# Down projections as Strassen block products in a two-block network

## The chip, the cores and the metric

The kernel runs on one core of one Trainium2 chip. The metric is the time of one execution on the device in microseconds (us). TensorE (PE in the rows; PEld is its weight load) multiplies matrices, VectorE (DVE), ScalarE (ACT) and GpSimd (POOL) work element by element, and SyncE (SP) issues the transfers. All weights come from device memory once per use; SBUF holds the operands and PSUM the sums of the matmuls.

## The reference

Two transformer blocks run one behind the other over 528 tokens (16 learned ones and 512 of the input) of width 1024. The first has two layers of mixed attention and a gated feed-forward net, the second one layer of sparse attention and a gated feed-forward net. The change concerns only the last product of each of the three feed-forward nets, the down projection from 2816 to 1024:

```python
def conv_ffn(x, w_up, conv_w, conv_b, w_down):
    h = x @ w_up
    ...
    u, g = jnp.split(hc, 2, axis=-1)
    return (jax.nn.silu(g) * u) @ w_down
...
h = h + conv_ffn(rms_norm(h, ffn_norm[i]), w_up[i], conv_w[i], conv_b[i], w_down[i])
...
h = h + (jax.nn.silu(f @ w_gate[i]) * (f @ w_up[i])) @ w_down[i]
```

Everything is float32.

## The kernel before

**Layout.** Features lie on the 128 partitions and tokens along the free axis. The residual h is eight tiles of 128 x 528; a feed-forward net has 22 tiles of 128 hidden features. Every operand of a matmul is split into a rounded part (hi) and a remainder (lo), and a product is three passes: hi by hi, hi by lo, lo by hi.

**Jobs.** The work on TensorE is a list of jobs. A job makes one block of 128 output features: `steps` (L304) runs over its K row blocks of the weights, and for each issues the three passes (L322) over the tokens. In layer 0 the tokens are two halves of 264 (`FULL`), each a matmul of its own with its own weight load; where the first 16 tokens are not needed, one matmul has all 512 (`SEQT`). The sum stands in one of two PSUM buffers `mm` and the job's `evac` takes it out. `load` (L247) brings weights for two jobs (a chunk `raw`, up to 1024 rows by 256 columns, 1 MB) into one of two buffers. `split` (L258) makes hi on ACT (L273) and lo on DVE (L274) from it; `run` (L337) calls it two jobs ahead of the job that needs it, and weights have three buffers each.

**The feed-forward nets.** The 22 hidden tiles are taken in thirds (`THIRDS`, L34: 8, 7 and 7 tiles). The order of jobs is: up projections of the first third and four jobs of the second, down projection of the first third, the rest of the second and four jobs of the last, down projection of the second third, the rest, down projection of the last third. A down projection of one third is a down phase here: eight jobs with K = 7 or 8, one per tile of h, each added to h by one DVE operation (L1035 in the layers, L1452 in block 2). After the last phase of a layer each tile of h is also scaled into the next stage's operands (L182, L193) and its squares are added up on POOL (L204). An up job ends with an evacuation with the norm's factor (L378), in the layers a convolution (L992 on ACT, L994 and L995 on DVE), the gate (L1006, L1008) and hi and lo of the product (L1010, L179); in block 2 with a gate on ACT (L1420) and POOL (L1421). In block 2 the last third is done twice, over 256 tokens each (the last stage: 16 jobs, L1470 takes out the sums, L1480 adds squares on POOL), so that one half's output work runs beside the other's matmuls.

**What sets the order.** The Python code is in program order, evacuations have a high priority, and a scheduler fixes each engine's queue when the program is built. Each engine then runs its queue strictly in order and waits at its head. The profile names tiles by their base: raw, wh, wl (weights), g (any 128 x 528 tile), mm (PSUM).

## Time and profile before

| what | value |
|---|---|
| median of 3 runs | 2361.13 us (2360.93 to 2361.45) |
| profiled execution | 2361.31 us |
| its span, first to last instruction | 2359.5 us |
| PE busy | 2318.5 us (98%) |
| VectorE busy | 1378.4 us (58%) |
| ScalarE busy | 952.2 us (40%) |
| GpSimd busy | 248.3 us (11%) |
| mean granted TensorE clock | 0.992 of full speed |
| read from device memory | 192.26 MB |

Busy times are sums over the span. Matmuls overlap in the pipeline, so PE counts as busy through most of the span, and the distance between starts is what one costs. The groups of instructions name the line, the tiles, the shapes and the number, the busy time, the mean duration of one, and the idle time of the engine ahead of them with what ended it. The table of stretches has one line for each stretch of the span: its length, the busy time and the number of instructions of PE, PEld, DVE, ACT and POOL in this order, the granted clock, the share of the transfer engines and their rate; its last line is the sum over the stretches asked for.

### The profile page before, as it was taken

What the parts mean: (1) busy time and instruction counts of PE and PEld (TensorE: products, weight loads), DVE (VectorE), ACT (ScalarE), POOL (GpSimd) and SP (SyncE); (2) the same over time, 40 slices, a digit from 0 to 9 for tenths busy, and PEclk for the clock granted to TensorE, in tenths of its full rate; (3) what the DMA queues carried; (4) which work ended last, traced back from release to release, by engine and by line L of the source; (5) the groups of instructions that cost most, each with busy time, mean ns of one, the idle gap of its engine ahead of it and who ended that gap; (6) DMA issues with size and microseconds to landing.
All of it is one profiled execution on the core that took longest, in us unless ns stands there. A gap on an engine that the chain in (4) does not pass through costs nothing.

```text
span 2359.5 us, 37628 instructions
## 1 busy us (share of the span) xinstructions
PE 2318.5 (98%) x15703; PEld 2133.4 (90%) x15703; DVE 1378.4 (58%) x2480; ACT 952.2 (40%) x1641; POOL 248.3 (11%) x261
## 2 busy tenths in 40 slices
PE   7999999999999999999999999999999999999998
PEld 6999999999998998999998889988999888888888
DVE  6667556465556677466464666797454454333335
ACT  6555434233346655343242544322233533222225
POOL 3111210000021112200000121100000002101012
PEclk9999999999999999999999999999999999999999
DMA  4211122222231211222223222222212222232323
GB/s 115 73 55 55 55 90 90 90 90 89 96 87 54 55 55 54 90 90 90 90 84 105 85 76 88 90 90 90 89 55 72 72 90 90 92 105 89 98 85 130
DMA packets 217072, 196.77 MB, mean 83 GB/s; under 512 B 8987, under 2 KB 214791, under 8 KB 216903
## 3 DMA queue, kind: packets, MB, share of 16 engines
q1 hardware_dynamic: 216903, 194.37, 25.9%
q8 instruction: 124, 2.03, 0.3%
q14 instruction: 45, 0.37, 0.1%
HBM read 192.26 MB, written 2.10 MB: 82 GB/s over the span
## 4 chain that ended last, share of the span: by engine, by line
PE 66%; ACT 1%; DVE 1%; issue 1%; POOL 0%; DMA 0%; POOLq 0%; ACTq 0%; SPq 0%
PE mm L322 59%; PE valuesT L1158 1%; PE scoresS L1141 1%; PE foxV L620 1%; PE attend_pT L480 1%; PE foxT L600 0%; ACT wh L273 0%; PE foxS L510 0%; POOL g L204 0%; PE spreadS L223 0%; PE foxS L511 0%; PE idx L510 0%; DMA raw<-in_w_down_dram 0%; PE to_tokensT L463 0%; PE idx L511 0%
## 5 line engine op out<-in xcount | busy, mean ns | idle before, releaser
L322 PE MATMUL mm<-g,wh 128*128 128x264 f32 (+3 forms) x9168 | 1883.0, 316 | 13.8 <-DVE g L378 11.7
L322 PEld LDWEIGHTS mm<-g,wh 128*128 128x128 f32 x9168 | 1393.3, 190 | 113.8 <-issue 12.8
L322 PE MATMUL mm<-g,wl 128*128 128x264 f32 (+3 forms) x4552 | 1161.0, 313 | 0.0
L322 PEld LDWEIGHTS mm<-g,wl 128*128 128x128 f32 x4552 | 752.2, 189 | 50.4
L273 ACT ACTIVATE wh<-raw 128x1024 fp32r<-128x1024 f32 (+1 forms) x369 | 384.9, 1043 | 947.9 <-PE mm L322 808.8
L274 DVE TENSOR_TENSOR wl<-raw,wh 128x1024 fp32r<-128x1024 f32 (+1 forms) x369 | 445.1, 1206 | 66.0 <-ACT wh L273 55.8
L378 DVE TENSOR_TENSOR g<-mm,g 128x528 f32<-128x528 f32 (+2 forms) x228 | 158.5, 696 | 318.7 <-PE mm L322 315.4
L204 POOL TENSOR_TENSOR g<-g,g 128x528 f32<-128x528 f32 (+3 forms) x49 | 71.4, 1469 | 914.9 <-ACT g L203 568.0
L179 DVE TENSOR_TENSOR g<-g,g 128x512 fp32r<-128x512 f32 (+3 forms) x131 | 92.1, 703 | 38.2 <-ACT g L1010 29.0
L1035 DVE TENSOR_TENSOR g<-mm,g 128x528 f32<-128x528 f32 (+1 forms) x48 | 33.6, 700 | 119.3 <-PE mm L322 119.3
L992 ACT ACTIVATE g<-g,cv 128x528 f32<-128x528 f32 (+1 forms) x88 | 72.1, 819 | 17.8 <-DVE g L378 17.7
L1421 POOL TENSOR_TENSOR g<-g,g 128x512 f32<-128x512 f32 x22 | 38.9, 1766 | 283.9 <-ACT g L1420 283.9
L995 DVE SCALAR_TENSOR_TENSOR g<-g,cv,g 128x526 f32<-128x526 f32 (+1 forms) x88 | 66.9, 760 | 3.1
L994 DVE SCALAR_TENSOR_TENSOR g<-g,cv,g 128x527 f32<-128x527 f32 (+1 forms) x88 | 66.3, 754 | 1.8 <-ACT g L992 1.8
L179 DVE TENSOR_TENSOR g<-foxT,g 128x128 fp32r<-128x128 f32 (+1 forms) x160 | 50.5, 340 | 20.3 <-ACT g L605 18.0
L1006 ACT ACTIVATE g<-g 128x528 f32<-128x528 f32 (+1 forms) x44 | 28.1, 639 | 84.0 <-DVE g L995 84.0
L1008 DVE TENSOR_TENSOR g<-g,g 128x528 f32<-128x528 f32 (+1 forms) x44 | 30.8, 701 | 32.4 <-ACT g L1006 32.4
L575 ACT ACTIVATE g<-g,sm 128x144 f32<-128x144 f32 (+2 forms) x80 | 43.1, 538 | 16.0 <-DVE sm L571 15.3
L187 POOL TENSOR_TENSOR sm<-sm,mhalf 128x10 f32<-128x10 f32 (+3 forms) x29 | 37.2, 1290 | 115.2 <-DVE sm L186 114.9
L605 ACT ACTIVATE g<-foxT 128x256 fp32r<-128x256 f32 (+1 forms) x96 | 33.1, 345 | 27.6 <-PE foxT L600 22.5
L1010 ACT ACTIVATE g<-g 128x528 fp32r<-128x528 f32 (+1 forms) x44 | 28.1, 638 | 33.1 <-DVE g L1008 33.1
L1452 DVE TENSOR_TENSOR g<-mm,g 128x512 f32<-128x512 f32 x16 | 11.1, 692 | 49.9 <-PE mm L322 49.9
(282 smaller groups left out, 1706.8 us busy)
## 6 DMA issues: line engine op xcount, KB each, us to landing
raw<-in_w_up_dram SPq DMA_DIRECT2D x50, 1024.0 KB
raw<-in_w_in_dram SPq DMA_DIRECT2D x44, 1024.0 KB
raw<-in_w_down_dram SPq DMA_DIRECT2D x28, 896.0 KB
raw<-in_w_in_dram SPq DMA_DIRECT2D x28, 512.0 KB
raw<-in_w_out_dram SPq DMA_DIRECT2D x12, 1024.0 KB
raw<-in_w_down_dram SPq DMA_DIRECT2D x12, 1024.0 KB
raw<-in_w_gate_dram SPq DMA_DIRECT2D x10, 1024.0 KB
raw<-in_w_up_dram SPq DMA_DIRECT2D x10, 512.0 KB
```

What stands on the lines that cost most here:

```text
L179: (eng or self.nc.vector).tensor_tensor(out, x, hi.bitcast(F32), op=ALU.subtract)
L187: self.nc.gpsimd.tensor_tensor(out, v[:rows, :n], self.mhalf[:rows, :n], op=ALU.pow)
L204: nc.gpsimd.tensor_tensor(acc[:, t0:t1], tmp[:, t0:t1], acc[:, t0:t1], op=ALU.add)
L273: keep(nc.scalar.activation(hi[:, :K], src, AF.Copy))
L274: keep(nc.vector.tensor_tensor(lo[:, :K], src, hi[:, :K].bitcast(F32), op=ALU.subtract))
L322: nc.tensor.matmul(ps[:, b, :n], lhsT=w[:, k, :], rhs=x[:, t:t + n], start=(ki == 0 and pi == 0), stop=(ki == len(order) - 1 and pi == len ...
L378: self.nc.vector.tensor_tensor(self.v(out, toks), self.psv(ps, toks), self.v(rs, toks), op=ALU.mult)
L575: nc.scalar.activation(P[:qs, :N], P[:qs, :N], AF.Exp, scale=-1.0, bias=m, accum_out=col)
L992: nc.scalar.activation(A[:, lo:], U[:, lo:], AF.Identity, bias=self.vec("cb", 44 * i + t), scale=cw(2))
L994: nc.vector.scalar_tensor_tensor(A[:, s1:], U[:, s1 - 1:L - 1], cw(1), A[:, s1:], op0=ALU.mult, op1=ALU.add)
L995: nc.vector.scalar_tensor_tensor(A[:, s0:], U[:, s0 - 2:L - 2], cw(0), A[:, s0:], op0=ALU.mult, op1=ALU.add)
L1421: nc.gpsimd.tensor_tensor(z[:, META:], z[:, META:], self.rs[:, META:], op=ALU.mult)
```

## The change

The down projections of all phases but block 2's last stage are done on pairs of output blocks. For two column blocks (128 features each), a pair of row blocks and the two token halves A and B, the 2 x 2 block product takes seven block products in place of eight. Line numbers of this section are those of the changed kernel.

- `THIRDS` is now 8, 8 and 6 tiles, so that row blocks pair up. Block 2's last stage keeps the plain form, with 6 row blocks.
- Weights: `split_product` makes the sums of weight blocks once per chunk: s1 on DVE (L279), s3 in place in `raw` and s2 and s4 on POOL (L280 to L282), then for each of the products 1, 6, 5, 7, 4, 2, 3 hi on ACT (L287) and lo on DVE (L288), each of n x 128 columns with n = 4 (or 3 in the third of 6).
- Hidden tiles: `seven` (L291) makes four differences of each tile pair (L296 to L299; on POOL, for the very last pair on DVE) and splits b11, t1 to t4, b21 and b22 (L301 to L308; the lo parts are L183).
- Products: `pair_steps` (L313) issues 3 n matmuls per product over one token half (L332), into PSUM tiles mmS (products 1, 6 and 4) and mm (5 with 7, 2 with 3). Sums of products are added to the two tiles h1 and h2 of the residual by ACT (L344), DVE with a PSUM input (L347, L349, L354, L357, L360) and POOL (L345, L350, L351).
- `run` (L448) cuts products ahead as long as six weight buffers hold them, and loads up to two chunks ahead. A job of the other kind takes two of the six buffers.
- Unchanged operations stand at other lines: L179, L182, L204, L274, L378, L994, L995 and L1008 of before are L183, L186, L208, L378, L516, L1132, L1133 and L1146 now.

```diff
-THIRDS = [list(range(0, 8)), list(range(8, 15)), list(range(15, 22))]
+THIRDS = [list(range(0, 8)), list(range(8, 16)), list(range(16, 22))]
+WTILES = 6
+
+PRODS = {1: ("a11", "b11"), 6: ("s2", "t2"), 5: ("s1", "t1"), 7: ("s3", "t3"), 4: ("a22", "t4"),
+         2: ("a12", "b21"), 3: ("s4", "b22")}
...
+    def split_product(self, jb, q):
...
+            nc.vector.tensor_tensor(s1, a21, a22, op=ALU.add)
+            nc.gpsimd.tensor_tensor(a21, a21, a11, op=ALU.add)
+            nc.gpsimd.tensor_tensor(s2, a21, a22, op=ALU.add)
+            nc.gpsimd.tensor_tensor(s4, s2, a12, op=ALU.add)
+            jb["left"] = dict(a11=a11, a12=a12, a22=a22, s1=s1, s2=s2, s3=a21, s4=s4)
+        src = jb["left"][PRODS[q][0]]
...
+        nc.scalar.activation(hi, src, AF.Copy)
+        nc.vector.tensor_tensor(lo, src, hi.bitcast(F32), op=ALU.subtract)
...
+    def seven(self, f1, f2, t0, n, eng):
...
+        eng.tensor_tensor(t12[:, :n], f1[:, B], f1[:, A], op=ALU.subtract)
+        eng.tensor_tensor(t12[:, n:2 * n], f2[:, B], t12[:, :n], op=ALU.subtract)
+        eng.tensor_tensor(t34[:, n:2 * n], f2[:, A], t12[:, n:2 * n], op=ALU.subtract)
+        eng.tensor_tensor(t34[:, :n], f1[:, B], f2[:, B], op=ALU.subtract)
...
+    def pair_steps(self, jb, prods):
...
+        for k in range(len(rhs)):
+            for q in prods:
+                hi, lo = jb["w"][q]
+                xh, xl = rhs[k][PRODS[q][1]]
+                for pi, (w, x) in enumerate(((hi, xh), (hi, xl), (lo, xh))):
+                    nc.tensor.matmul(z[q], lhsT=w[:, k, :], rhs=x, start=k == 0 and pi == 0,
+                                     stop=k == len(rhs) - 1 and pi == 2)
...
+                if q == 1:
+                    z["u"], z["v"] = self.G(), self.G()
+                    nc.scalar.activation(z["u"][:, :n], z[1], AF.Copy)
+                    nc.gpsimd.tensor_tensor(h1[:, A], h1[:, A], z["u"][:, :n], op=ALU.add)
+                elif q == 6:
+                    nc.vector.tensor_tensor(z["v"][:, :n], z[6], z["u"][:, :n], op=ALU.subtract)
+                elif q == 5:
+                    nc.vector.tensor_tensor(z["v"][:, n:2 * n], z[5], z["v"][:, :n], op=ALU.add)
+                    nc.gpsimd.tensor_tensor(h2[:, t0:t0 + 2 * n], h2[:, t0:t0 + 2 * n], z["v"][:, :2 * n], op=ALU.add)
+                    nc.gpsimd.tensor_tensor(h1[:, B], h1[:, B], z["v"][:, n:2 * n], op=ALU.subtract)
+                elif q == 7:
+                    hv = h2[:, t0:t0 + 2 * n].rearrange("p (a b) -> p a b", a=2)
+                    nc.vector.tensor_tensor(hv, z[7].unsqueeze(1).to_broadcast([128, 2, n]), hv, op=ALU.add)
...
+    def units(self, jb):
+
+        if not jb.get("pair"):
+            return [(jb, None, 1 if jb.get("packed") else 2)]
+        groups = [[1, 6, 5, 7], [2], [3], [4]] if jb.get("first") else [[q] for q in PRODS]
+        return [(jb, g, len(g)) for g in groups]
```

**DVE's queue in a full down phase.** The queue of VectorE in the first down phase of layer 0, before: one evacuation (L1035) and one split (L274) per job.

```order
L1035 TENSOR_TENSOR g29_216<-mm948_5436,g29_216 128x528
L274 TENSOR_TENSOR wl950_5487<-raw938_5320,wh949_5486 128x1024
L1035 TENSOR_TENSOR g36_234<-mm951_5490,g36_234 128x528
L274 TENSOR_TENSOR wl954_5543<-raw945_5430,wh953_5542 128x1024
L1035 TENSOR_TENSOR g42_254<-mm955_5546,g42_254 128x528
```

The same phase of the changed kernel, between two L347 (of the third and the fourth column pair). g1011 is s2, g1010 s1, g1012 s4, made in this stretch.

```order
L279 TENSOR_TENSOR g1010_5698<-raw990_5552 128x512
L288 TENSOR_TENSOR w1013_5705<-raw990_5552,w1013_5705 128x512
L349 TENSOR_TENSOR g1006_5676<-mm1014_5708,g1006_5676 128x264
L288 TENSOR_TENSOR w1015_5724<-g1011_5699,w1015_5724 128x512
L354 TENSOR_TENSOR g50_278<-mm1014_5708,g50_278 128x528
L288 TENSOR_TENSOR w1016_5740<-g1010_5698,w1016_5740 128x512
L360 TENSOR_TENSOR g50_278<-mmS_1017_5743,g50_278 128x264
L288 TENSOR_TENSOR w1018_5757<-raw990_5552,w1018_5757 128x512
L288 TENSOR_TENSOR w1020_5773<-raw990_5552,w1020_5773 128x512
L357 TENSOR_TENSOR g42_254<-mm1019_5760,g42_254 128x528
L288 TENSOR_TENSOR w1021_5789<-raw990_5552,w1021_5789 128x512
L288 TENSOR_TENSOR w1025_5809<-g1012_5700,w1025_5809 128x512
```

Per column pair the queue has thirteen operations (with the L347) in place of four, and splits of the fourth pair's products stand between evacuations of the third's.

**The start of a phase.** VectorE's queue in the changed kernel from the evacuation of the last up job (the row ahead of the first shown, L516) to the first L347 of the phase. w966, w967 and w971 are weights of products 4, 2 and 3 of the first column pair, w977 of product 1 of the second; the rows of L183 are remainders of `seven`'s sums of an up tile pair.

```order
L288 TENSOR_TENSOR w966_5396<-raw920_5042,w966_5396 128x512
L288 TENSOR_TENSOR w967_5399<-raw920_5042,w967_5399 128x512
L1132 SCALAR_TENSOR_TENSOR g956_5369<-g955_5367,cv_135,g956_5369 128x527
L288 TENSOR_TENSOR w971_5419<-g946_5244,w971_5419 128x512
L1133 SCALAR_TENSOR_TENSOR g956_5369<-g955_5367,cv_135,g956_5369 128x526
L288 TENSOR_TENSOR w977_5445<-raw940_5185,w977_5445 128x512
L1146 TENSOR_TENSOR g956_5369<-g956_5369,g943_5238 128x528
L183 TENSOR_TENSOR g959_5381<-g951_5306,g959_5381 128x264
L183 TENSOR_TENSOR g961_5385<-g957_5375,g960_5384 128x528
L183 TENSOR_TENSOR g963_5389<-g958_5376,g962_5388 128x528
L183 TENSOR_TENSOR g965_5393<-g956_5369,g964_5392 128x528
L347 TENSOR_TENSOR g970_5416<-mmS_973_5424,g969_5415 128x264
```

Before, the place had one split, the two conv steps, the product and one remainder ahead of the first evacuation.

**POOL's queue in the same phase.** Before, GpSimd has nothing in a layer between the sums of squares of the stage ahead and those behind the feed-forward net; in the changed kernel a column pair has these six (here the weight adds of the fourth pair and the output adds of the third, the last row of the fourth).

```order
L280 TENSOR_TENSOR raw990_5552<-raw990_5552 128x4x128
L281 TENSOR_TENSOR g1011_5699<-raw990_5552 128x512
L350 TENSOR_TENSOR g50_278<-g50_278,g1006_5676 128x528
L351 TENSOR_TENSOR g42_254<-g42_254,g1006_5676 128x264
L282 TENSOR_TENSOR g1012_5700<-g1011_5699,raw990_5552 128x512
L345 TENSOR_TENSOR g56_303<-g56_303,g1023_5805 128x264
```

POOL goes from 266 to 570 rows in its queue, DVE from 2382 to 2738.

## Rows read from the trace of the kernel before

**Rows 1.** The page's engine totals: busy us, share of the span, instructions.

```profile
PE 2318.5 (98%) x15703; PEld 2133.4 (90%) x15703; DVE 1378.4 (58%) x2480; ACT 952.2 (40%) x1641; POOL 248.3 (11%) x261
```

**Rows 2.** Table of stretches, down phases: busy us (number) per engine, clock, DMA share, GB/s.

```profile
432.00:478.70 46.70, 46.70 (x386) 46.70 (x385) 18.50 (x21) 10.48 (x12) 0.00 (x0) 1.00 0.28 91
...
1105.40:1150.10 44.70, 44.70 (x195) 36.14 (x195) 18.60 (x22) 10.63 (x12) 0.00 (x0) 1.00 0.28 93
...
sum 334.70, PE 333.71 PEld 292.96 DVE 150.72 ACT 102.27 POOL 31.34; mean PE 41.71 PEld 36.62 DVE 18.84 ACT 12.78 POOL 3.92
```

**Rows 3.** Groups of DVE, stretch 432.0 to 478.7, the first down phase of layer 0.

```profile
L274 DVE TENSOR_TENSOR wl<-raw,wh 128x1024 fp32r<-128x1024 f32 x8 | 9.8, 1224 | 0.9
L1035 DVE TENSOR_TENSOR g<-mm,g 128x528 f32<-128x528 f32 x8 | 5.7, 707 | 25.8 <-PE mm L322 25.8
```

**Rows 4.** Timeline of PE, last stage: start us, us, operation, number.

```profile
2313.22 0.28 PE L322 MATMUL mm<-g,wl 128*128 128x256 f32 x1
2313.34 0.40 PE L322 MATMUL mm<-g,wh 128*128 128x256 f32 x2
2313.57 0.28 PE L322 MATMUL mm<-g,wl 128*128 128x256 f32 x1
2313.69 0.39 PE L322 MATMUL mm<-g,wh 128*128 128x256 f32 x2
2313.93 0.28 PE L322 MATMUL mm<-g,wl 128*128 128x256 f32 x1
```

**Rows 5.** Groups by shape over the whole span: splits, evacuations, a conv step, ACT.

```profile
L274 DVE TENSOR_TENSOR wl<-raw,wh 128x1024 fp32r<-128x1024 f32 x313 | 384.0, 1227 | 56.3 <-ACT wh L273 48.8
L274 DVE TENSOR_TENSOR wl<-raw,wh 128x896 fp32r<-128x896 f32 x56 | 61.1, 1091 | 9.7 <-ACT wh L273 7.0
L378 DVE TENSOR_TENSOR g<-mm,g 128x528 f32<-128x528 f32 x96 | 67.3, 703 | 97.8 <-PE mm L322 96.7 <-ACT g L225 1.0
L995 DVE SCALAR_TENSOR_TENSOR g<-g,cv,g 128x526 f32<-128x526 f32 x44 | 33.8, 767 | 1.6
L1008 DVE TENSOR_TENSOR g<-g,g 128x528 f32<-128x528 f32 x22 | 15.6, 708 | 17.0 <-ACT g L1006 17.0
L1420 ACT ACTIVATE g<-g 128x512 f32<-128x512 f32 x22 | 13.7, 622 | 0.0
L1470 DVE TENSOR_TENSOR g<-mm,g 128x256 f32<-128x256 f32 x16 | 6.8, 425 | 2.5 <-PE mm L322 1.1
```

**Rows 6.** Timeline, block 2's up jobs: POOL alone, then with a split.

```profile
1986.60 1.29 POOL L1421 TENSOR_TENSOR g<-g,g 128x512 f32<-128x512 f32 x1 [6.25 <-ACT g L1420]
...
1988.81 1.22 DVE L274 TENSOR_TENSOR wl<-raw,wh 128x1024 fp32r<-128x1024 f32 x1 [0.21 <-ACT wh L273]
1989.37 1.82 POOL L1421 TENSOR_TENSOR g<-g,g 128x512 f32<-128x512 f32 x1 [1.48 <-ACT g L1420]
```

**Rows 7.** Timeline, layer 1's attention: a split issued behind a POOL operation.

```profile
728.69 1.18 POOL L427 TENSOR_TENSOR c<-g,g 8x528 bf16<-8x528 f32 x1
728.78 2.17 DVE L274 TENSOR_TENSOR wl<-raw,wh 128x1024 fp32r<-128x1024 f32 x1
```

**Rows 8.** Timeline, last stage: an evacuation beside a POOL add.

```profile
2335.53 0.77 POOL L1480 TENSOR_TENSOR g<-g,g 128x256 f32<-128x256 f32 x1 [4.13 <-ACT g L1477]
...
2336.08 0.43 DVE L1470 TENSOR_TENSOR g<-mm,g 128x256 f32<-128x256 f32 x1 [0.17 <-PE mm L322]
```

**Rows 9.** Timeline, last stage: a POOL add with DVE idle.

```profile
2346.48 0.73 POOL L1480 TENSOR_TENSOR g<-g,g 128x256 f32<-128x256 f32 x1 [1.51 <-ACT g L1477]
```

**Rows 10.** Table of stretches: eight up jobs of layer 0.

```profile
340.00:386.80 46.80, 46.80 (x387) 46.80 (x386) 32.13 (x41) 19.69 (x24) 0.00 (x0) 1.00 0.28 91
```

**Rows 11.** Groups by shape: ACT's splits of the down weights with K = 7.

```profile
L273 ACT ACTIVATE wh<-raw 128x896 fp32r<-128x896 f32 x56 | 53.4, 953 | 122.2 <-PE mm L322 108.8 <-issue 12.1 <-DMA raw<-in_w_down_dram 1.2
```

**Rows 12.** Table of stretches: a gap of PE in layer 0, and behind it.

```profile
255.00:259.00 4.00, 0.51 (x3) 0.36 (x2) 3.25 (x5) 2.00 (x3) 0.00 (x0) 0.88 0.03 11
259.00:263.00 4.00, 4.00 (x20) 4.00 (x20) 0.74 (x3) 0.82 (x2) 0.00 (x0) 0.50 0.01 4
```

More of the change, by code (lines that the diff above doesn't have):

```diff
@@ L256, in load, with wtile, pair_job @@
         ch["raw"] = raw
+    def wtile(self):
+        return self.wp.tile([128, 1024], F32R, tag="w", name=self.n("w"))
+    def pair_job(self, ch, rhs, t0, n, out, done):
+        self.jobs.append(dict(ch=ch, rhs=rhs, t0=t0, n=n, out=out, done=done, side=[], w={}, pair=True))
+    def split_product(self, jb, q):
+        nc, ch = self.nc, jb["ch"]
+        self.load(ch)
+        n = ch["K"] // 2
+        if "left" not in jb:
+            v = ch["raw"][:, :2 * n].rearrange("p (k z) c -> p z k c", z=2)
+            a11, a12, a21, a22 = [v[:, z, :, 128 * x:128 * x + 128] for x in range(2) for z in range(2)]
+            s1, s2, s4 = [self.G()[:, :128 * n].rearrange("p (k c) -> p k c", k=n) for _ in range(3)]
+            nc.vector.tensor_tensor(s1, a21, a22, op=ALU.add)
[4 more added lines that the diff above has]
+        src = jb["left"][PRODS[q][0]]
+        w = self.wtile()
+        hi, lo = [w[:, o:o + 128 * n].rearrange("p (k c) -> p k c", k=n) for o in (0, 512)]
+        nc.scalar.activation(hi, src, AF.Copy)
+        nc.vector.tensor_tensor(lo, src, hi.bitcast(F32), op=ALU.subtract)
+        jb["w"][q] = (hi, lo)
@@ L270, in split @@
         src = ch["raw"][:, :K, jb["off"]:jb["off"] + 128]
-        hi = self.wp.tile([128, 8, 128], F32R, tag="wh", name=self.n("wh"))
-        lo = self.wp.tile([128, 8, 128], F32R, tag="wl", name=self.n("wl"))
+        hi, lo = [self.wtile().rearrange("p (k c) -> p k c", k=8) for _ in range(2)]
         keep(nc.scalar.activation(hi[:, :K], src, AF.Copy))
@@ L335, in steps @@
                 jb["evac"](ps)
-    def run(self, look=2, ahead=4):
-        n = len(self.jobs)
-        self.credit, self.late = 0.0, None
-        i = 0
-        while i < n:
-            g = self.jobs[i:i + 2] if i == 0 else self.jobs[i:i + 1]
-            for q in range(i, min(i + ahead + 1, n)):
-                self.load(self.jobs[q]["ch"])
-            for q in range(i, min(i + len(g) + (look if i else 0), n)):
-                if self.jobs[q]["w"] is None:
-                    self.split(self.jobs[q], pin=i < 2)
-            for jb in g:
-                for s in jb["side"]:
-                    s()
-                if jb.get("flush"):
-                    self.drain_pipe()
-                    self.pump(10 ** 6)
-                self.rate = jb.get("rate", self.rate)
-            gens = [self.steps(jb) for jb in g]
+    def units(self, jb):
[3 more added lines that the diff above has]
+        return [(jb, g, len(g)) for g in groups]
@@ new lines, in run, with loads, cut_to @@
+    def run(self):
+        self.credit, self.late = 0.0, None
+        units = [u for jb in self.jobs for u in self.units(jb)]
+        chunks = []
+        for jb, _, _ in units:
+            if not any(c is jb["ch"] for c in chunks):
+                chunks.append(jb["ch"])
+        left = {id(c): sum(u[0]["ch"] is c for u in units) for c in chunks}
+        cut = [2]
+        def loads():
+            used = sum(left[id(c)] == 0 for c in chunks)
+            for c in chunks[:used + 2]:
+                self.load(c)
+        def cut_to(u):
+            jb, g, _ = units[u]
+            if g is None:
+                self.split(jb)
+            else:
+                for q in g:
+                    self.split_product(jb, q)
+            left[id(jb["ch"])] -= 1
+            loads()
+        for u in range(2):
+            left[id(units[u][0]["ch"])] -= 1
+        u = 0
+        while u < len(units):
+            g = units[u:u + 2] if u == 0 else units[u:u + 1]
+            if u:
+                while cut[0] < len(units) and sum(x[2] for x in units[u:cut[0] + 1]) <= WTILES:
+                    cut_to(cut[0])
+                    cut[0] += 1
+            else:
+                loads()
+            gens = []
+            for jb, prods, _ in g:
+                if prods is None or 1 in prods:
+                    for s in jb["side"]:
+                        s()
+                    if jb.get("flush"):
+                        self.drain_pipe()
+                        self.pump(10 ** 6)
+                    self.rate = jb.get("rate", self.rate)
+                gens.append(self.steps(jb) if prods is None else self.pair_steps(jb, prods))
```

117 lines of the change are left out of this document (84 added, 33 removed).

## The prediction

> **What bounds the kernel now.** I read the page's engine totals first: TensorE (PE) is busy for 98% of the span, VectorE (DVE) for 58%, GpSimd (POOL) for 11% [rows 1]. Then the table of stretches for the eight down phases that the change rewrites, counted from evacuation to evacuation: they last 334.7 us together, PE is busy in all but one microsecond of them, and POOL does nothing in most [rows 2]. In the first phase DVE runs only eight weight splits and eight evacuations and waits 25.8 us for PE [rows 3]. So each phase lasts as long as its matmuls: 386 in 46.70 us is 0.121 us per matmul of 264 columns; 195 in 44.70 us is 0.229 per 512 columns [rows 2]. In the last stage, which already has 256 columns per matmul with a weight load each, six start within 0.71 us, 0.118 each [rows 4]. Half the columns thus cost half the time, and the extra weight loads in layer 1 and block 2 are free as far as the rows show.
>
> **The change on PE.** A pair of output column blocks over n pairs of row blocks takes 7 x 3 x n matmuls of half the tokens. A full phase (n = 4, four column pairs) has 336: 40.7 us at 264 columns, 39.6 at 256. A phase with n = 3 has 252: 30.5 or 29.7. The thirds are now 8, 8, 6 row blocks, so six phases have n = 4 (two per layer, two in block 2) and two n = 3. On PE alone: 2 x 40.7 + 30.5 + 4 x 39.6 + 29.7 = 300.0 against 334.7. The last stage isn't Strassen, but it has 6 row blocks in place of 7: 3 matmuls fewer in each of 16 jobs, 48 x 0.118 = 5.7 us less, with nothing against it. If PE stays the bound, 40.4 us go.
>
> **What DVE and POOL get in exchange.** Durations from the grouped rows: a DVE split took 1.227 us for 1024 elements and 1.091 for 896, so about 0.69 for 512 and 0.55 for 384; an evacuation from PSUM 0.703 for 528, 0.425 for 256; ACT 0.62 for 512 [rows 5]. A POOL add of 512 elements took 1.29 when DVE left it alone [rows 6], one of 256 took 0.73 [rows 9]; 384 I put between, at 1.0. Per column pair with n = 4 DVE now has one add (L279) and seven splits (L288), 5.5 us, and five evacuations, 2.7 us: 8.2 us, where it had 3.9 (two of each). POOL had none and gets three weight adds (L280 to L282) and three adds for the output (L345, L350, L351): 4 x 1.29 + 2 x 0.73 = 6.6 us. ACT has 7 x 0.62 and a copy, under 5 us, and stays covered by PE's 9.9 to 10.2.
>
> DVE and POOL don't run these side by side. A POOL add met by a split in progress took 1.82 us in place of 1.29 [rows 6]: it waited for the split. A split issued 0.09 us behind a POOL operation of 1.18 us took 2.17 in place of 1.23 [rows 7]: it waited too. An evacuation, whose one input is PSUM, ran in its usual 0.43 us beside POOL [rows 8]. So two-SBUF-input work on DVE and POOL's adds exclude each other: 5.5 + 6.6 = 12.1 us per column pair, against 9.9 on PE. The rows also show what a handover saves, since the waiting side has started up: POOL 1.82 - 0.66 = 1.16 after the split's end, 0.13 less than alone; DVE 1.08 after POOL's end, 0.15 less. With 0.28 per POOL add the sum is 10.4.
>
> The Trainium skill (SBUF — State Buffer, section "SBUF: two separate sides") speaks against this change: it calls the pair of ports an exclusive lock, held for the full instruction by whichever side starts first. The trace agrees, but for that handover; by the rule alone the sum is 12.1, by the rows 10.4.
>
> **One column pair, step by step.** DVE takes its queue in order; the first order excerpt shows a pair's queue between two L347. From the start of L347: evacuation to 0.43, L279 to 1.1, first split to 1.8, L349 to 2.2. L280 may overwrite its rows only after L279 has read them; it gets the ports at 1.8 and ends at 3.0, L281 ends at 4.25, ACT's rounding at 4.9. The split that needs it (L288 from L281's sum) waits at DVE's head meanwhile. POOL's L350, next in its queue (third excerpt), has taken the ports at 4.25 and holds them to 5.5, so that split ends at 6.0. Then L354, a split, L282 on POOL (1.15 more), a split at 9.1, and one split, L357 and two splits at 0.69 each: 11.8; L345 of the next pair costs some 0.4 more. I take **12 us per column pair**, and 11 for the first turn, some of whose splits stand ahead. DVE, not PE (10), sets that pace. Without any lock the same queue still has the chain L347, L279, L280, L281, ACT, split: 5.4 us, and 5.3 of work behind it: 10.7.
>
> **A phase.** At its start the queue ahead of the first L347 (second excerpt) holds an evacuation 0.70, four splits 2.8, two conv steps of 0.77, a product and three splits of 0.71, one of 0.37: 8.2 us, and POOL's work for the last up tiles (four times 0.75, L282 1.29) blocks some 3.4 of it: 11.6. PE has five products ready, 60 x 0.121 = 7.3 us, and then needs a PSUM buffer that L344 or L347 frees. Then come turns of 11, 12 and 12, and 1.5 us for the last product: **48.1 us** for n = 4. With n = 3: queue at the start 9.0 (the sums of the last tiles are on DVE); a turn 12 - 8 x 0.14 - 3 x 0.29 = 10.0, plus two scaled splits (L186) of 0.76 and some 0.8 of POOL's squares, 12.4; end 3.1: 9.0 + 37.2 + 3.1 = **49.3 us**. In layer 1 POOL has more squares, 11.3 us of its own per pair, which still fits 12.4.
>
> Sum: 6 x 48.1 + 2 x 49.3 = 387.2, against 334.7: 52.5 us more; less 5.7: 46.8 more. The profiled execution took 2361.3 (0.2 over the median): **2408 us**.
>
> **Costed at nothing.** The seven sums of each tile pair in the up phases (L296 to L308): 3 us on POOL and 1.1 more on DVE in 23.4, where DVE is busy 32.1 of 46.8 us and POOL idle [rows 10]; without that cover up to 4 us per pair of tiles. The loads: same bytes, a column pair per 10 to 12 us as now, a DMA share of 0.28 [rows 2], and the splits of down weights waited 1.2 us in all for them [rows 11]; SP issues a load when the chunk two before it is split, as the two raw buffers allowed before. Weight buffers: six as before; a product is split five products ahead, about 7 us. The squares that trail the last down phase of a layer, some 8 us: the next stage's first evacuation needs them, and two PSUM buffers hold two jobs, 11 us; without that, up to 5 us per layer.
>
> **Rivals.**
> (1) *PE stays the bound.* If POOL's adds slip into DVE's evacuations and DVE's 8.2 us per pair hide under PE's 9.9, the saving of 40.4 stays: **2321 us**. It decides when a turn falls under 9.9. For it: DVE is busy only 18.5 of 46.7 us of a phase now [rows 2]. Against it: the 10.4 of the ports alone, and the chain of 10.7. The Trainium skill (Perfetto Trace Analysis, "Identifying the Most-Contended Engine") would take this view: it says to optimize the engine with the highest occupancy first, here PE. The occupancies agree; the eight phases are another regime.
> (2) *The ports are packed well.* Turns of 10.5 and a start of 10: n = 4 takes 43.0, n = 3 (9 + 31.5 + 3.1) 43.6; 345.2 in all, +10.5 - 5.7: **2366 us**. For it: POOL runs ahead when it is not queued behind L350. Against it: one queue order, fixed at build.
> (3) *The clock.* After 3.5 us without matmuls the granted clock was 0.50, the lower level of 1.2 GHz, for the next stretch [rows 12]. A start stall of nearly 4 us in each of eight phases may cost 3.4 us each behind it, 27 us: **2435 us**. Against it: PE has slack while DVE sets the pace.
> The change not doing what it says is excluded: the order of the built program has 21 matmuls per n and pair.
>
> **Chances.** Forecast 0.52 (own range 2385 to 2432), rival 1 0.17 (2321 to 2345), rival 2 0.21 (2350 to 2385), rival 3 0.10. The range 2345 to 2442 leaves out rival 1 and a tail of rival 3. 0.2%, about what a measurement of this kernel tells from no change, is 4.7 us: rival 2 gives 0.07 to "same" and 0.05 to "faster", rival 1 all of its 0.17 to "faster". Faster 0.22, same 0.07, slower 0.71.
>
> **What would show it.** Right: in the down phases PE idles before L332 for splits (L288) and for L347 or L344; DVE splits of 512 elements average well over 0.69 us and POOL's adds over 1.29; a pair takes about 12 us; the phases about 48. Wrong: PE busy through the phases and splits at 0.69 us (rival 1); long waits of L287 for raw would mean the loads.

## The result and the profile after

The changed kernel takes **2446.4 us** (median of four runs, 2445.5 to 2446.9) against 2361.0 (2360.3 to 2361.5): a ratio of **1.036, interval [1.034, 1.038]**, 85 us slower. The prediction was slower, 2408 us with a range to 2442; the direction came, and 38 us more. The profiled execution took 2445.46 us, its span 2443.7. Single executions of one kernel here lie up to 5 us from the median (before: 2357 to 2365 in later runs), so no difference of that size between two totals is read below, unless both are medians of several executions. Runs 2 to 10 are one execution each; beside runs 9 and 10 the kernel before took 2364.4 us in its one execution.

Engine totals of the page after, to set beside [rows 1]:

```profile
PE 2322.7 (95%) x16231; PEld 2161.5 (88%) x16231; DVE 1590.4 (65%) x2836; ACT 1038.7 (43%) x1893; POOL 585.9 (24%) x565
```

PE issues more matmuls (16231 for 15703) but is busy only 4 us longer; the rest of the added time is waiting. Table of stretches of the eight down phases, each from its first matmul to its last (columns as in [rows 2]: length, busy PE, PEld, DVE, ACT, POOL with their numbers, granted clock, DMA share, GB/s):

```profile
430.60:483.50 52.90, 45.66 (x340) 44.11 (x339) 39.65 (x58) 21.91 (x38) 29.89 (x25) 0.94 0.25 80
...
676.50:732.00 55.50, 42.37 (x255) 39.17 (x254) 47.40 (x69) 23.53 (x50) 30.85 (x26) 0.82 0.19 53
...
1384.20:1442.40 58.20, 40.62 (x262) 37.12 (x260) 46.62 (x75) 30.89 (x69) 34.81 (x32) 0.88 0.21 65
2168.30:2218.60 50.30, 43.17 (x338) 41.87 (x337) 36.70 (x53) 20.05 (x35) 28.39 (x24) 0.97 0.26 84
2307.60:2350.80 43.20, 40.91 (x338) 40.09 (x337) 32.29 (x50) 19.02 (x32) 28.54 (x21) 1.00 0.30 98
sum 417.40, PE 345.76 PEld 330.47 DVE 320.54 ACT 180.72 POOL 241.72; mean PE 43.22 PEld 41.31 DVE 40.07 ACT 22.59 POOL 30.22
```

The phases took 334.7 us [rows 2] and now take 417.4: 82.7 of the 84.2 us by which the span grew. The two with n = 3, which have a quarter less work, are the longest (55.5 and 58.2). The last one, block 2's second, is the only one shorter than eight row blocks would be plainly (8 jobs x 24 x 0.229 = 44.0).

**How a phase starts.** Timeline of PE and ACT, first phase (start us, us, engine, line, operation, number, idle time before and what ended it):

```profile
439.26 0.64 ACT L307 ACTIVATE g<-g 128x528 fp32r<-128x528 f32 x1 [1.40 <-POOL g L297]
440.66 1.18 ACT L307 ACTIVATE g<-g 128x528 fp32r<-128x528 f32 x2 [0.76 <-POOL g L298]
441.74 0.37 ACT L344 ACTIVATE g<-mmS 128x264 f32<-128x264 f32 x1
...
442.17 3.67 PE L332 MATMUL mmS<-g,w 128*128 128x264 f32 x15 [4.08 <-ACT g L344]
```

Product 1, twelve matmuls of 0.121 from 430.6 on, was done at 432; its copy L344 stands in ACT's queue behind the three roundings of `seven` (L307), which wait for POOL's differences. PE waits 4.08 us for it. So it is ACT's queue that stalls the start, and not DVE's, which the prediction had named; the length, 12.0 us to the first L347, is near the 11.6 predicted.

**A turn** (from one L347 to the next). Timeline of DVE and POOL in the second turn of the same phase (L347 at 452.89 and 465.74):

```profile
454.77 1.81 DVE L279 TENSOR_TENSOR g<-raw 128x512 f32<-128x512 f32 x1
456.51 1.24 DVE L288 TENSOR_TENSOR w<-raw,w 128x512 fp32r<-128x512 f32 x1
457.67 0.69 DVE L354 TENSOR_TENSOR g<-mm,g 128x528 f32<-128x528 f32 x1
...
460.96 1.83 DVE L288 TENSOR_TENSOR w<-g,w 128x512 fp32r<-128x512 f32 x2 [2.07 <-ACT w L287]
...
454.33 1.70 POOL L350 TENSOR_TENSOR g<-g,g 128x528 f32<-128x528 f32 x1 [3.11 <-DVE g L349]
456.00 1.19 POOL L351 TENSOR_TENSOR g<-g,g 128x264 f32<-128x264 f32 x1
457.16 1.75 POOL L280 TENSOR_TENSOR raw<-raw 128x512 f32<-128x512 f32 x1
458.98 1.28 POOL L281 TENSOR_TENSOR g<-raw 128x512 f32<-128x512 f32 x1
```

Both mechanisms of the prediction stand here: L279 takes 1.81 us and ends 0.55 behind POOL's L350, a split 1.24 and ends 0.56 behind L351, while L354, with its input in PSUM, runs in its usual 0.69 beside POOL; and at 460.96 the split of s2 has held DVE's head for 2.07 us until L281 and ACT were done.

**The last phase of layer 1.** Timeline at its end:

```profile
1436.25 7.78 POOL L208 TENSOR_TENSOR g<-g,g 128x528 f32<-128x528 f32 x6 [4.85 <-ACT g L207]
1443.99 0.72 POOL L345 TENSOR_TENSOR g<-g,g 128x256 f32<-128x256 f32 x1
1444.67 1.25 POOL L350 TENSOR_TENSOR g<-g,g 128x512 f32<-128x512 f32 x1
1445.89 0.72 POOL L351 TENSOR_TENSOR g<-g,g 128x256 f32<-128x256 f32 x1
...
1446.64 0.69 DVE L357 TENSOR_TENSOR g<-mm,g 128x512 f32<-128x512 f32 x1 [3.91 <-POOL g L351]
...
1447.48 2.90 PE L426 MATMUL mm<-g,w 128*128 128x512 f32 x6 [5.07 <-DVE g L357]
```

Six adds of squares stand in POOL's queue ahead of the output adds, DVE waits 3.91 us for these, and PE 5.07 us for a PSUM buffer, so that even the next stage's first matmul is late.

### The profile page after: what moved, and what is told of

Read it like the earlier page. It is cut to its first block, busy times and chain, and to the rows that moved or that the text cites. A ratio compares the mean times of both kernels' runs of the same rounds, so it can differ in the third digit from the quotient of the medians.

```text
span 2443.7 us, 39954 instructions
## 1 busy us (share of the span) xinstructions
PE 2322.7 (95%) x16231; PEld 2161.5 (88%) x16231; DVE 1590.4 (65%) x2836; ACT 1038.7 (43%) x1893; POOL 585.9 (24%) x565
## 4 chain that ended last, share of the span: by engine, by line
PE 74%; DVE 9%; POOL 6%; issue 6%; ACT 4%; DMA 1%; SPq 0%; POOLq 0%; ACTq 0%; DVEq 0%
PE mm L426 61%; PE mm L332 3%; DVE w L288 3%; POOL raw L280 1%; PE foxV L758 1%; POOL g L281 1%; PE mmS L332 1%; PE valuesT L1299 1%; POOL g L208 1%; PE foxT L738 1%; DVE w L378 1%; DVE g L183 1%; ACT w L287 1%; PE scoresS L1282 1%; POOL g L350 1%
## 5 line engine op out<-in xcount | busy, mean ns | idle before, releaser
L426 PE MATMUL mm<-g,w 128*128 128x264 f32 (+3 forms) x11728 | 1820.2, 312 | 21.8 <-DVE g L516 13.9
L426 PEld LDWEIGHTS mm<-g,w 128*128 128x128 f32 x11728 | 1621.4, 190 | 132.8 <-issue 20.3
L377 ACT ACTIVATE w<-raw 128x1024 fp32r<-128x1024 f32 (+1 forms) x305 | 319.4, 1048 | 639.2 <-PE mm L426 531.1
L378 DVE TENSOR_TENSOR w<-raw,w 128x1024 fp32r<-128x1024 f32 (+1 forms) x305 | 372.9, 1223 | 54.7 <-ACT w L377 48.7
L516 DVE TENSOR_TENSOR g<-mm,g 128x528 f32<-128x528 f32 (+2 forms) x228 | 158.2, 694 | 246.2 <-PE mm L426 242.8
L332 PE MATMUL mm<-g,w 128*128 128x256 f32 (+1 forms) x1440 | 207.9, 299 | 29.7 <-DVE g L349 16.0
L332 PEld LDWEIGHTS mm<-g,w 128*128 128x128 f32 x1440 | 194.0, 203 | 37.2 <-DVE g L349 21.1
L332 PE MATMUL mmS<-g,w 128*128 128x256 f32 (+1 forms) x1080 | 161.0, 297 | 41.9 <-ACT g L344 19.5
L332 PEld LDWEIGHTS mmS<-g,w 128*128 128x128 f32 x1080 | 145.7, 199 | 49.5 <-ACT g L344 22.4
L183 DVE TENSOR_TENSOR g<-g,g 128x512 fp32r<-128x512 f32 (+5 forms) x191 | 139.0, 741 | 47.9 <-ACT g L307 38.1
L287 ACT ACTIVATE w<-g 128x512 fp32r<-128x512 f32 (+1 forms) x96 | 54.4, 596 | 183.4 <-POOL g L281 179.1
L208 POOL TENSOR_TENSOR g<-g,g 128x528 f32<-128x528 f32 (+3 forms) x49 | 73.4, 1511 | 209.2 <-ACT g L207 209.2
L288 DVE TENSOR_TENSOR w<-g,w 128x512 fp32r<-128x512 f32 (+1 forms) x96 | 80.1, 841 | 58.0 <-ACT w L287 58.0
L296 POOL TENSOR_TENSOR g<-g 128x256 f32<-128x256 f32 (+1 forms) x28 | 21.2, 759 | 337.7 <-DVE g L1146 314.9
L288 DVE TENSOR_TENSOR w<-raw,w 128x512 fp32r<-128x512 f32 (+1 forms) x128 | 99.9, 799 | 0.2 <-ACT w L287 0.2
L287 ACT ACTIVATE w<-raw 128x512 fp32r<-128x512 f32 (+1 forms) x128 | 73.5, 594 | 24.0 <-PE mm L426 11.8
L1132 DVE SCALAR_TENSOR_TENSOR g<-g,cv,g 128x527 f32<-128x527 f32 (+1 forms) x88 | 67.4, 765 | 17.0 <-ACT g L1130 16.9
L307 ACT ACTIVATE g<-g 128x512 fp32r<-128x512 f32 (+1 forms) x90 | 54.0, 629 | 55.2 <-POOL g L297 39.7
L1133 DVE SCALAR_TENSOR_TENSOR g<-g,cv,g 128x526 f32<-128x526 f32 (+1 forms) x88 | 72.0, 818 | 2.3
L280 POOL TENSOR_TENSOR raw<-raw 128x512 f32<-128x512 f32 (+1 forms) x32 | 48.8, 1525 | 83.0 <-DVE g L279 31.5
```

The costliest lines, as they stand in the source:

```text
L183: (eng or self.nc.vector).tensor_tensor(out, x, hi.bitcast(F32), op=ALU.subtract)
L208: nc.gpsimd.tensor_tensor(acc[:, t0:t1], tmp[:, t0:t1], acc[:, t0:t1], op=ALU.add)
L280: nc.gpsimd.tensor_tensor(a21, a21, a11, op=ALU.add)
L287: nc.scalar.activation(hi, src, AF.Copy)
L288: nc.vector.tensor_tensor(lo, src, hi.bitcast(F32), op=ALU.subtract)
L332: nc.tensor.matmul(z[q], lhsT=w[:, k, :], rhs=x, start=k == 0 and pi == 0, stop=k == len(rhs) - 1 and pi == 2)
```

## The experiments

Two theories at the start: **the ports and DVE's queue** (two-SBUF-input work of DVE and POOL's adds exclude each other) set the pace of the phases; or **PE itself**, by half-width matmuls or by the clock behind the start stalls. Beside them, the wait chain through L281 as a cause apart from the amount of port work. Line numbers in the rows of an experiment are those of its own kernel; names are given where they differ.

**1. The thirds alone.** The kernel before with

```diff
-THIRDS = [list(range(0, 8)), list(range(8, 15)), list(range(15, 22))]
+THIRDS = [list(range(0, 8)), list(range(8, 16)), list(range(16, 22))]
```

> The kernel before with the thirds 8, 8, 6 and plain down projections. My sum says that only the last stage gets shorter, 48 matmuls of 256 columns x 0.118 us = 5.7 us, and that the row blocks only move between the other stages: 2355.4 us. Rival: the end is set by the output work behind the last sums and not by matmuls, 2361 us.

Measured: 2360.5 us, ratio 0.9995 [0.9986, 1.0004]. The expectation had forgotten that block 2's second third gets an eighth row block: 8 jobs x 3 x 0.229 = 5.5 us, which take back the 5.7. So the run doesn't test the last stage, but it shows that the thirds are worth nothing by themselves: all 85 us are the block products'. (In the prediction's sum the eighth row block was counted, in the 300.0.)

**2. Without the weight sums.**

```diff
-            s1, s2, s4 = [self.G()[:, :128 * n].rearrange("p (k c) -> p k c", k=n) for _ in range(3)]
...
-            nc.gpsimd.tensor_tensor(s4, s2, a12, op=ALU.add)
+            s1, s2, s4 = a21, a22, a12
```

> The changed kernel without the four weight sums of a column pair (L279 to L282): s1, s2 and s4 are replaced by raw blocks, so the products 6, 5, 7 and 3 are of other matrices, and everything else stays. If DVE's queue and its exclusion with POOL set the pace, both lose work (DVE 0.7, POOL 3.9 us per pair), a turn falls to PE's own 10.2 us in the full phases (3.9 us less per phase of three turns, six phases) and by some 3 us per turn in the two phases with n = 3: about -42 us, 2404 us. If PE's half-width matmuls or its clock set the pace, the turns stay and it is 2440 us or more.

Measured: 2403.1 us. Stretch of the first phase:

```profile
430.90:477.90 47.00, 43.57 (x340) 42.86 (x339) 34.84 (x53) 22.27 (x37) 16.86 (x16) 0.96 0.27 90
```

The second and third turn of the full phases fall to 10.1 to 10.4 us, PE's own, the first to 7.3 to 7.6 in five of them; all eight phases together to 367.7. PE's matmuls are as cheap as predicted: the sums, four instructions per pair, cost 43 us. The run takes away port work and the wait for L281 at once, so it doesn't tell which of the two it was.

**3. `seven` behind the first pair's second product.**

```diff
+                    if self.defer:
+                        self.defer()
+                        self.defer = None
```

(behind L347 of `pair_steps`; `defer` holds the call for the tile pair just finished)

> The changed kernel, but where a full phase starts, the four differences and seven roundings of the up tile pair just finished (not needed before the next phase) are issued behind the second product of the phase in place of ahead of it. If the start stall comes from L344 standing in ACT's queue behind these roundings, PE's idle 4.1 us ahead of L344 go in the four full phases of the layers and most of the half-clock stretch behind each (3.4 us of work): -16 to -30 us, 2416 to 2430 us; block 2, which starts sooner, gains little. Rival: the work only moves into the first turn, which the ports bound anyway: 2440 us or more.

Measured: 2455.3 us, 9 us slower than the changed kernel. The start fell as expected, from 12.0 to 7.0 us in the first phase, but the first turn rose from 10.3 to 15.9 and the second from 12.8 to 14.1. The rival holds: a start that is freed of work passes it to a turn that has no room. The start stall was not a loss of its own.

**4. The weight sums earlier.**

```diff
                 for q in g:
                     self.split_product(jb, q)
+                nx = units[u + 3][0] if u + 3 < len(units) else jb
+                if nx is not jb and nx.get("pair") and nx["ch"]["raw"] is not None:
+                    self.weight_sums(nx)
```

(`weight_sums` is the part of `split_product` that makes s1 to s4)

> The changed kernel, with the four weight sums of the next column pair issued some three products earlier, behind the split of the fifth product of the pair before. The same work on every engine. If the head-of-line wait (DVE's split for product 6 waits for ACT, ACT for POOL's L281, POOL for DVE's L279) makes the turns long, a turn falls from 11.5 to about 10.5 us: -20 to -40 us, 2406 to 2426 us. If the sum of port work alone makes them long, or PE, it stays within 8 us of 2446.

Measured: 2477.2 us, 31 us slower than the changed kernel and outside both expected values. Stretches of the first two turns of the first phase:

```profile
448.38:460.57 12.19, 11.04 (x73) 10.31 (x73) 10.47 (x14) 3.49 (x7) 8.75 (x7) 0.85 0.24 81
460.57:472.65 12.08, 10.80 (x86) 10.37 (x85) 10.97 (x13) 4.47 (x9) 8.65 (x6) 1.00 0.27 87
```

The wait for s2 is gone (DVE is busy for 10.97 of 12.08 us, its durations drawn out by POOL; one wait for ACT of 0.98 us is left), and the turn is 12.1 us all the same; the last turn, which has no sums, takes 7.9. The sums that this turn lost went into the start, now 17.4 us for 12.0. Over the eight phases the starts grew by 37 us and the turns fell by 11. So the wait of L288 for L281 was no cause of its own: without it, a turn with the same port work is no shorter. Why the moved sums cost more at the start than they give back at the end isn't shown.

**5. The weight sums on DVE.** 

```diff
-            nc.gpsimd.tensor_tensor(a21, a21, a11, op=ALU.add)
+            nc.vector.tensor_tensor(a21, a21, a11, op=ALU.add)
```

and so for s2 and s4.

> The changed kernel with the three weight adds of L280 to L282 on DVE in place of POOL. An add of 512 elements takes DVE about 0.69 us and POOL 1.29, so the work that excludes itself falls from 12.1 to 7.6 + 2.75 = 10.3 us per pair, and DVE alone then has 7.6 + 2.7 = 10.3. If the summed port work sets the turn, it falls from 11.5 to some 10.5 us in the full phases and by 2 to 3 us in the two with n = 3: -24 us, about 2422 us. If only DVE's own queue counts, its work grows by 2.1 us per turn: 2460 us or more.

Measured: 2425.9 us, near the port account's 2422. More work on the busier engine made the kernel 20.5 us faster. The account has the sum right and not its parts: the turns of the full phases fell by 0.5 us in the mean (206.5 to 197.4 us for 18) where 1 was expected, and the starts, which it left out, by 1.2 us each.

**6. All six adds on DVE.** As 5, and L345, L350 and L351 on `nc.vector` too.

> The changed kernel with all six adds of a pair (L280 to L282, L345, L350, L351) on DVE: nothing excludes DVE then in a full phase, and its own queue has 8.2 + 2.1 + 1.5 = 11.8 us per turn. By the port account that is a little more than the 11.5 measured with POOL's help: 2446 to 2465 us. If what makes the turns long is the waiting between the two engines and not the amount of work, turns fall towards 10.2: 2410 us.

Measured: **2404.5 us**, 42 us faster than the changed kernel, where my port account had said no gain. Stretches of two turns of the first phase, and of the first full phases of layer 1 and the second of block 2:

```profile
447.83:458.68 10.85, 10.84 (x87) 10.54 (x86) 10.85 (x21) 4.42 (x9) 0.00 (x0) 1.00 0.29 98
458.68:469.34 10.66, 10.66 (x88) 10.45 (x87) 10.28 (x21) 4.41 (x9) 0.00 (x0) 1.00 0.31 100
...
1126.60:1172.00 45.40, 41.58 (x340) 40.45 (x339) 43.59 (x78) 19.95 (x36) 2.91 (x4) 1.00 0.28 93
2270.40:2310.60 40.20, 40.20 (x338) 39.99 (x338) 38.74 (x71) 18.45 (x32) 0.00 (x0) 1.00 0.33 106
```

The turn isn't 11.8 but 10.7 to 10.85, in layer 1 and block 2 mostly 10.2, and in the turns shown PE is busy throughout. Timeline of DVE in the first of these turns:

```profile
448.18 1.28 DVE L288 TENSOR_TENSOR w<-raw,w 128x512 fp32r<-128x512 f32 x2
449.38 0.42 DVE L349 TENSOR_TENSOR g<-mm,g 128x264 f32<-128x264 f32 x1
449.73 0.68 DVE L288 TENSOR_TENSOR w<-g,w 128x512 fp32r<-128x512 f32 x1
450.33 0.70 DVE L350 TENSOR_TENSOR g<-g,g 128x528 f32<-128x528 f32 x1
```

A split lasts 0.68 us, but the next operation starts 0.60 behind it (449.73 to 450.33; two splits in 1.20), an evacuation lasts 0.42 and costs 0.35. My account had added durations, and so made DVE 10 to 15% dearer than it is: the 19 operations of a turn are 11.7 us by durations and 10.2 by starts. At 10.2 the amount of work gives the same turn as the rival (the waiting between the engines), so this run doesn't part the two; runs 4 and 10 do. And block 2's second phase takes 40.2 us, PE busy throughout at the full clock: the price of its matmuls, predicted at 39.6, is right.

**7. The third of six tiles plain in the layers.**

```diff
-                self.pair_job(ch, lambda: [act[t // 2] for t in ts[::2]], D0, DN, HP(k), done(x, k))
+                if x < 2:
+                    self.pair_job(ch, lambda: [act[t // 2] for t in ts[::2]], D0, DN, HP(k), done(x, k))
+                    continue
+                for b in range(2):
+                    self.job(ch, 128 * b, lambda: [act[t] for t in ts], TD, ev_down(k + b, done(x, k), b))
```

> The changed kernel, but the third of six tiles in the two layers is done plainly (seven() and the block products stay in the first two thirds). Eight jobs of 18 row-block passes take 34.9 us at two times 264 columns and 33.0 at 512, where the block products took 55.5 and 58.2; and the 5 us that each stage behind them started late (5.1 and 4.9 us more between the phases of layer 0, layer 1 and block 2 than before) go, if they are the squares and splits that trail the last phase: -46 - 10, about 2390 us. If they have another cause, 2400 us.

Measured: 2396.9 us, 49.5 less, between the two guesses. Two of the eight phases, with what they delay behind them, carry more than half of the change's 85 us. In the trace the stretch behind layer 1's last phase, up to the next net's first phase, is back at 720.5 us (725.9 in the changed kernel, 720.7 before); that behind layer 0 is not (409.3, 410.1 and 404.8). So both guesses were half right.

**8. PE kept busy through the start stall.**

```diff
+                if k == 0 and q in (5, 7) and jb.get("twice"):
+                    for kk in range(len(rhs)):
...
+                            nc.tensor.matmul(z[q], lhsT=w[:, kk, :], rhs=x, start=kk == 0 and pi == 0,
+                                             stop=kk == len(rhs) - 1 and pi == 2)
```

> The changed kernel with the products 5 and 7 of the first pair issued twice in the four full phases of the layers, 2.9 us of matmuls more, which lie in PE's 4.1 us of waiting for L344; the result is the same. If the half-clock stretches behind the start stall cost time, they go or shorten, and each of these phases gets 1.5 to 3.4 us shorter: 2433 to 2440 us. If DVE and the ports set the pace, PE's clock is covered and the phases stay within 1 us: 2446 us.

(`twice` is set for the first pair of these four phases.) Measured: 2452.2 us, above both expected values. Stretches of layer 0's two full phases:

```profile
432.10:486.50 54.40, 47.99 (x364) 47.03 (x363) 38.81 (x58) 22.05 (x38) 28.78 (x25) 0.94 0.24 78
579.80:634.20 54.40, 45.46 (x363) 44.26 (x362) 38.84 (x58) 21.94 (x38) 28.82 (x25) 1.00 0.23 78
```

They are the same work, on the first and on the second third. In the first the granted clock was at its lower level, 1.2 GHz, for 6.8 us behind the stall (0.94 over the phase), in the second at 2.4 GHz throughout: both last 54.4 us, and PE's 2.5 us more are taken from its waiting. In the changed kernel both were at 0.94 and took 52.9 and 53.0 us. In layer 1 the clock of the two phases stayed at 0.97, so this one phase at 1.00 is the whole of the test. None of the four got shorter (the doubled products made each 1.0 to 1.5 us longer), so in layer 0's full phases the clock isn't what is paid for. The n = 3 phases, at 0.82 and 0.88 in the changed kernel, were not tested.

**9. Squares left out.** In the last phase of the two layers (here layer 0's; the three calls of layer 1 likewise):

```diff
-                    self.sq_acc(nxt["acc2"], h, new)
+                    self.sq_acc(nxt["acc2"], h, new, add=False)
```

> The changed kernel without POOL's adds of squares (L208) in the last phase of the two layers (ACT still squares; the norms behind use the first tile's squares alone). These adds are two per column pair in layer 0 and four wide and two narrow ones in layer 1. If they take the ports in the turns with n = 3, those get 2 us shorter in layer 0 and 4 to 5 us in layer 1, and the 5 us that the stages behind start late go too: -6 - 13 - 8, about 2420 us. If the scaled splits on DVE and their wait for ACT set these turns, the time falls by under 8 us: 2440 us.

Measured: 2428.6 us, 18 less, between the two expected values. In layer 0 the three turns fall from 38.9 to 33.8 us, near what was expected of POOL adds on the ports (6). In layer 1 they don't fall (45.8 to 47.1): the norm of the next stage no longer waits for the sums, its small steps moved up into DVE's and POOL's queues ahead of L347, and the run says nothing of the squares there.

**10. POOL adds that nobody reads.** The kernel of 6 with

```diff
+                    for _ in range(2):
+                        nc.gpsimd.tensor_tensor(self.G()[:, :2 * n], z["v"][:, :2 * n], z["v"][:, :2 * n], op=ALU.add)
```

> The run with all six adds of a pair on DVE (2404.5 us), with two adds per pair given to POOL that nobody reads, of 528 or 512 elements from v to spare tiles. No instruction waits for their results. If POOL's adds keep DVE off its two-SBUF-input work, each costs a turn up to 1.1 us (1.29 less the handover) where it doesn't fall on an evacuation: +40 to +64 us over 32 pairs, 2445 to 2468 us. If what POOL's adds cost the changed kernel was only the waiting for their results, these cost nothing: 2404 us.

Measured: 2443.1 us, 38.6 more than 6, just under the range of the port theory and far from the rival's nothing. Stretches of the first phase in run 6 and in this run, and timeline at the end of its first turn:

```profile
428.20:475.80 47.60, 44.32 (x339) 42.99 (x339) 44.16 (x78) 20.48 (x37) 2.97 (x4) 0.96 0.27 89
431.40:483.80 52.40, 45.30 (x340) 43.32 (x339) 49.47 (x78) 20.40 (x36) 16.10 (x12) 0.97 0.25 80
```

```profile
450.04 1.56 DVE L288 TENSOR_TENSOR w<-raw,w 128x512 fp32r<-128x512 f32 x1
451.52 1.29 DVE L345 TENSOR_TENSOR g<-g,g 128x264 f32<-128x264 f32 x1
452.73 0.42 DVE L347 TENSOR_TENSOR g<-mmS,g 128x264 f32<-128x264 f32 x1
...
449.66 2.86 POOL L353 TENSOR_TENSOR g<-g 128x528 f32<-128x528 f32 x2 [9.91 <-DVE w L288]
```

One split and one add, 0.68 and 0.42 us in 6, take 1.56 and 1.29 beside POOL's two adds. In this phase no instruction waits for one of its eight adds, and it takes 4.8 us more than in 6: that is the exclusion, by itself, 0.6 us per add. On the whole it is 38.6 / 64 = 0.6 too, but there another cause is mixed in: no instruction reads the adds' results, yet in 7 of the 32 pairs L347 waits for an L353, 11.1 us in all, perhaps for a tile that the add still holds.

**11 and 12. What is left when the ports are free.** The kernel of 6 with the plain third of 7; and the same with `seven` of the pair that is done as a net's first phase starts called behind product 6 of that phase's last column pair, where no weights are left to cut:

```diff
+                    if self.defer and jb.get("last"):
+                        self.defer()
+                        self.defer = None
```

> The run with all six adds on DVE, and with the third of six tiles in the two layers plain. The phases of that third take 34.9 + 33.0 us plain where they took 51.6 + 60.0 with all adds on DVE: -43.7; some 4 us more go behind them, as in the run with the plain third alone (49.5 us less, of which its two phases gave 45.8): 2404.5 - 48 = 2357 us, within 0.2% of the kernel before. If the six adds on DVE delay the up jobs (their evacuations stand in the same queue), 2362 us or more.

> As the run before, and the differences and roundings of the tile pair that is finished as the first phase of a net starts (three places) are issued behind product 6 of the last column pair of that phase. L344 then has nothing on ACT ahead of it that waits, and DVE has 2.3 us less ahead of the first L347 while no weights are left to cut at the end: the starts fall by 3 to 4 us in three phases, 2346 to 2349 us. If the ports only pass the delay on, as in the run that put the same work behind the first pair, 2357 us.

Measured: 2355.8 us, ratio to the kernel before 0.9977 [0.9968, 0.9985]; and **2349.45 us, 0.9951 [0.9937, 0.9964]**, the fastest of all. Stretches of the six phases of the second:

```profile
431.40:475.10 43.70, 42.88 (x342) 41.75 (x340) 43.38 (x77) 20.66 (x37) 4.80 (x4) 1.00 0.30 97
568.20:613.00 44.80, 42.71 (x340) 41.51 (x339) 42.46 (x77) 19.17 (x34) 0.00 (x0) 1.00 0.29 95
...
sum 257.10, PE 250.15 PEld 244.56 DVE 250.71 ACT 118.33 POOL 12.91; mean PE 41.69 PEld 40.76 DVE 41.79 ACT 19.72 POOL 2.15
```

The first phase of layer 0, 46.7 us plain [rows 2] and 52.9 in the changed kernel, is 43.7 here, and PE is busy for 250 of 257 us. Deferring `seven`, which lost in 3, where it landed on full turns, gains 6 us here, where it lands on a turn with room. So seven products do beat eight where PE is left as the bound.

## Why the prediction came out as it did

The sum of the prediction, term by term (us; six phases with n = 4, two with n = 3; the phases are divided at their first and last L347):

| term | predicted | measured |
|---|---|---|
| starts, n = 4 and n = 3 | 69.6 and 18.0 | 58.2 and 20.7 |
| turns, n = 4 and n = 3 | 210.0 and 74.4 | 206.5 and 84.7 |
| ends, n = 4 and n = 3 | 9.0 and 6.2 | 39.1 and 8.4 |
| eight phases | 387.2 | 417.4 |
| all else against before | -5.7 | +1.5 |

- **The step that failed is "and 1.5 us for the last product".** L347 takes out product 6, the second of seven. Five products of the last pair are still to come behind it, so the end is 5 x 12 x 0.121 = 7.3 us less what of them has run, not one product. Measured, in the first phase from the last L347 to the last matmul:

```profile
477.00:483.50 6.50, 6.50 (x54) 6.36 (x53) 4.22 (x7) 2.21 (x3) 2.94 (x2) 1.00 0.50 161
```

  54 matmuls, PE busy all the time. The end is 6.3 to 7.0 us in all six full phases, and 6.3 to 7.2 in the runs 2, 5 and 6 that took POOL's work away: it is plain PE work, left out of the sum. That is 30 of the 38 us missing. A count of the phase's PE time (40.7) beside the sum would have shown it: three turns contain only 21 of 28 products. That the rest misses by no more than 8 us is in part luck: starts forecast 8.7 us too long stand against turns 6.8 us and all else 7.2 us too short.
- **The turns of n = 4 are right** (34.4 predicted 35 in layer 0, 18 turns in all 206.5 for 210), by the mechanism named: run 10 shows the exclusion alone, 5 and 6 that less POOL work shortens the turn. Run 4 shows that the wait chain I built the 12 us from, L347 to L281 to ACT, isn't needed: decoupled, the turn is 12.1. The closeness of the number is partly luck: the turn's 13 operations on DVE start 0.08 us closer than they last (run 6), so with the right prices the same account would have had some 1 us less per turn. The Trainium skill (SBUF — State Buffer, section "SBUF: two separate sides") says that whichever of the two starts first holds the pair of ports for the whole instruction. By that rule I had 12.1 us, by the rows with their handover 10.4; the turns measured 11.5 in the mean and 12.1 in run 4, nearer the rule, though not to be taken as its proof to a tenth: DVE's operations are closer than I had them, and run 4's turn has 1 us of waiting in it.
- **The turns of n = 3 were mis-sized by 10 us** (12.4 each, though its terms add up to 12.3; measured 13.0 in layer 0, 15.3 in layer 1). "Some 0.8 of POOL's squares" was too little: run 9 gives 5.1 us in layer 0's three turns. In layer 1 I had let POOL's 11.3 us "fit" the turn by their sum; but in POOL's queue they stand in one piece of 7.8 us ahead of the output adds, for which DVE and then PE wait.
- **The starts** were right in the layers (11.7 to 12.1 for 11.6; 10.6 and 10.1 for 9.0) for a partly wrong reason (ACT's queue), and too long by 4 and 8 us in block 2, which has no conv steps ahead and, in its second phase, no `seven` either.
- **Costed at nothing:** `seven` beside the up jobs held (the stretches between a net's phases grew by nothing but the two up jobs moved). The trailing squares seemed not to: from the last matmul of a layer's last phase to the first phase of the next net it takes 5.1 and 4.9 us more than before, the "up to 5 us per layer" that was named as their price without cover. In layer 1 it is a wait, for a PSUM buffer that wasn't free. In layer 0 most of it is not. Stretches behind layer 0's last phase, before, in run 1 and in the changed kernel:

```profile
700.46:1105.23 404.77, 393.33 (x3178) 382.19 (x3177) 268.64 (x569) 205.50 (x423) 58.53 (x76) 0.99 0.23 70
700.58:1109.12 408.54, 397.18 (x3178) 386.14 (x3177) 268.72 (x569) 205.32 (x423) 58.49 (x76) 0.98 0.23 70
732.05:1142.10 410.05, 396.67 (x3178) 385.26 (x3178) 277.00 (x580) 208.43 (x433) 78.33 (x96) 0.98 0.23 70
```

  PE waits 13.4 us in place of 11.4; the other 3 us are the same matmuls at a lower mean clock, and run 1, with plain down projections, has them too. There the squares were covered but for some 2 us.
- **The last stage's -5.7** came: from block 2's last product to the end it is some 16.7 us less than before, of which two up jobs moved ahead are 11.
- **The rivals.** PE as the bound: not in this kernel, but its price of the products is right (40.2 us in run 6). Ports packed well: no. The clock: stretches at the lower level came in seven of eight phases; in layer 0's full ones they cost nothing that run 8 could find, and in the n = 3 phases their price stays open.
- **What was wrong in the account without hurting it:** DVE's work was summed from durations, where the starts are 0.08 us closer. That kept me from seeing that DVE alone could carry all six adds.

What stays open: layer 1's n = 3 turns (run 9 was disturbed there), and how much of the 4.9 us behind layer 1 is the squares' and how much the late output adds'.

## What to carry to other kernels

Before work goes to GpSimd because VectorE is busy, price it as time taken from VectorE's operations with two SBUF inputs: here an add of 512 elements took 1.29 us on GpSimd [rows 6] and takes 0.60 us on VectorE, and taking all six back made the kernel 42 us faster. When a phase is summed as start, turns and end, check that the pieces hold all its work on every engine; the term that nobody looked at was the one that missed. An arithmetic saving of an eighth on the bounding engine is only had where the other engines' new work fits under what is left of it: here with two of three thirds, with the adds on VectorE alone, and with the hidden tiles' preparation put where there is room; the kernel is then 0.5% faster than before.
